# A build-time clock that decides where constant products fill TensorE's gaps: busy share against array-weighted activity

## The chip, the cores and the metric

The kernel runs on one core of a Trainium2 chip. The metric is device time in microseconds of one execution, lower is better; the times given are medians of several runs.

## The reference

A two-layer encoder trunk runs over two groups of 512 tokens (width 1024, 16 heads of 64) with shared weights, all in float32:

```
for i in range(2):
    xn = rms_norm(x, pre_norm_g[i])
    h  = rwkv7_branch(xn) if i == 0 else natten_branch(xn)
    x  = x + rms_norm(h, post_norm_g[i])

# layer 0: r, k, v, z projections; per direction d (forward, backward):
S_t = S_{t-1} (diag(decay_t) + a_t b_t^T) + v_t k_t^T ;  y_t = S_t r_t
out = (group_norm(y_fwd + y_bwd) + bonus) * silu(z) @ w_o
# layer 1: q, k, v, z = xn @ w_in + b_in; attention over a window of 8 x 16 grid tokens
# with a learned relative bias; (o * silu(z)) @ w_o + b_o
```

The inputs are two activations of 512 x 1024 and the weights; the outputs are two activations of the same shape.

## The kernel before

Each 1024 x 1024 matrix is worked off as 8 columns of 8 blocks of 128 x 128 against 512 tokens. To keep float32 accuracy on a faster product, weights and activations are each split into a high part (a cast on ACT) and a low part (a subtraction on DVE), and each block is multiplied three times (lines 802 to 804 in the scan phase, 423 to 425 in the other two).

The program has three stages in time. A prelude normalises both groups, forms the shifted inputs and multiplies the first columns. The scan phase (`scan_phase`, line 1641) runs the recurrence of layer 0 in chunks of 64 tokens for 8 pairs of head groups, 64 steps in all, together with the rest of layer 0's columns and the first of layer 1's. The last stage (`rest`, line 1745) is attention and output.

In the scan phase the recurrence needs many small products. A step (`step`, line 1135) reads the state and the chunk in 64 x 64 products (lines 1162, 1168), copies Z on ACT (1174), solves with the inverse (1189), copies X (1201), and forms the next state and the output in 128 x 64 products (1209, 1213). The factors of the next step are 64 x 64 products too (1068, 1090). For every pair of head groups `prep` (line 823) forms the chunk operands, with two 128 x 128 products for each of four small matrices (872, 873) and Gram products of 64 x 32 (951), and `inverse` (line 975) inverts triangular blocks on DVE and joins them with products of 32 x 32 (lines 1025 and 1027, 64 in a group). Transposes (680, 1288) and sums (646, 1278) use 128 rows.

The order of instructions on TensorE, DVE and ACT in the scan phase is not left to the compiler. `weave` (line 1600) holds a list of generators, "threads": the step, its factors, the loads, the columns (`flow`, line 698), `prep`, `inverse`, `finish` (line 1237). Each yields the engine that it needs next and a function that says when its operands are ready. A class `Clock` keeps a model of time for each engine: every instruction that a thread issues is passed to `note`, which advances its engine and books when its outputs are made. Among the threads that are open and ready within 60 ns (`EPS`) `weave` takes the one of the lowest rank (the step is 0, the columns' products 9), lets it issue up to its next yield, and repeats. Times in this model come from formulas such as `0.4375 * n + 3` ns for a product of n columns in the split format and `1.73 * n + 1` for a full float32 one.

Where no thread is ready, `weave` may put a filler: a product of two constants, the identity (128 x 128) and 256 columns of a constant table, into a part of PSUM that nothing reads (`self.spare`, line 1154). The filler is on line 1626. Three conditions hold for it: no thread is ready, the next TensorE work of any open thread is over `WARM` = 300 ns away in the model, and `Clock.cool` says that TensorE did little in the last 3413 ns of model time. `Clock.busy` then books 440 ns for it. The model is only used at build time; on the chip the filler is an ordinary instruction in TensorE's order.

`cool` sums the intervals in the list `Clock.work`. Two places feed the list: `busy` for fillers, and `weave` after every step of a thread that moved TensorE's time, with the interval from its time before the step to the end of its last product. The tiles of the array are modelled in `matmul`: a product of fewer rows or columns than 128 has a `tile_size` and a `tile_position`, and two products run side by side if they share the column position and differ in the row position.

## Time and profile before

| | |
|---|---|
| median of 3 runs | 1694.72 us (1691.98 to 1698.94) |
| profiled execution, its own time | 1691.19 us |
| its span, first to last instruction | 1689.4 us |
| mean granted TensorE clock | 0.971 |
| TensorE busy | 1572.3 us (93%), 18820 products |
| fillers (line 1626) | 196 |

The profile is of one execution. PE is TensorE's products, PEld its weight loads, DVE the vector engine, ACT the scalar engine, POOL GpSimd, SP the engine that issues the DMAs. "Granted clock" is the share of full speed at which TensorE was clocked in a stretch. Rows of groups give the line, the engine, what is written from what, the shape, how often, then the busy time and the mean of one in nanoseconds, then the idle time of the engine before them and what ended it.

### The profile page before, as it was taken

The numbers are of one execution on the slowest core, as the hardware profiler recorded it, in microseconds if no ns is written. First come the engines' busy times: TensorE is split into PE (matmuls) and PEld (weight loads), VectorE is DVE, ScalarE is ACT, GpSimd is POOL, SyncE is SP. The second block draws the span as 40 slices with busy tenths as digits, with TensorE's granted clock in tenths as the row PEclk, the third lists the DMA queues.
The fourth block names the chain that finished last, engine by engine and source line by source line (L and its number), as shares of the span: only waits on it lengthen the run. The fifth ranks groups of instructions, "written<-read, shape, count | busy, mean of one in ns | idle before, by whom it ended". The sixth has DMA issues, their size and how long they took to land. (4 is left out here: it accounts for less than half of the span.)

```text
span 1689.4 us, 46296 instructions
## 1 busy us (share of the span) xinstructions
PE 1572.3 (93%) x18820; PEld 1201.0 (71%) x18820; DVE 1229.1 (73%) x2725; ACT 982.1 (58%) x1977; POOL 24.2 (1%) x94
## 2 busy tenths in 40 slices
PE   7989888899988998989988999999999898999998
PEld 5767666676766766767766767777787687777776
DVE  8985668689678787887888888745676766465564
ACT  5443655677765768656566665444676655555562
POOL 0000000000000000000000000000000000000000
PEclk9989999899999999999998999999999899999999
DMA  5435678688587787775776765554765246545553
GB/s 208 162 125 187 202 231 260 181 253 267 183 262 229 215 263 238 229 245 181 231 254 209 220 206 165 171 186 138 269 205 172 86 124 240 189 149 176 167 176 106
DMA packets 240821, 336.26 MB, mean 199 GB/s; under 512 B 53696, under 2 KB 119360, under 8 KB 240608
## 3 DMA queue, kind: packets, MB, share of 16 engines
q1 hardware_dynamic: 240608, 333.31, 61.9%
q8 instruction: 148, 2.42, 0.6%
q14 instruction: 65, 0.53, 0.1%
HBM read 227.71 MB, written 105.51 MB: 197 GB/s over the span
## 5 line engine op out<-in xcount | busy, mean ns | idle before, releaser
L802 PE MATMUL pm<-act,whi 128*128 128x512 f32 x640 | 284.9, 445 | 17.2 <-ACT act L747 4.3
L804 PE MATMUL pm<-act,wlo 128*128 128x512 f32 x640 | 258.0, 403 | 10.0 <-DVE wlo L723 9.9
L803 PE MATMUL pm<-act,whi 128*128 128x512 f32 x640 | 258.4, 404 | 7.4 <-DVE act L749 6.4
L423 PE MATMUL pg<-act,whi 128*128 128x512 f32 x448 | 184.0, 412 | 3.1 <-ACT os L1494 1.9
L424 PE MATMUL pg<-act,whi 128*128 128x512 f32 x448 | 179.2, 400 | 4.8 <-DVE act L373 4.8
L425 PE MATMUL pg<-act,wlo 128*128 128x512 f32 x448 | 179.0, 399 | 0.0
L372 ACT CAST whi<-raw 128x512 fp32r<-128x512 f32 x148 | 91.3, 618 | 131.1 <-PE pg L424 87.2
L802 PEld LDWEIGHTS pm<-act,whi 128*128 128x128 f32 x640 | 122.8, 192 | 62.2 <-issue 11.5
L804 PEld LDWEIGHTS pm<-act,wlo 128*128 128x128 f32 x640 | 123.4, 193 | 42.2 <-DVE wlo L723 15.1
L803 PEld LDWEIGHTS pm<-act,whi 128*128 128x128 f32 x640 | 123.5, 193 | 33.3 <-DVE act L749 12.4
L373 DVE TENSOR_TENSOR wlo<-raw,whi 128x512 fp32r<-128x512 f32 x148 | 101.7, 689 | 61.7 <-ACT whi L372 56.2
L723 DVE TENSOR_TENSOR wlo<-raw,whi 128x512 fp32r<-128x512 f32 x160 | 109.1, 685 | 36.5 <-ACT whi L721 33.2
L721 ACT CAST whi<-raw 128x512 fp32r<-128x512 f32 x160 | 98.4, 617 | 58.1 <-PE pm L803 27.5
L424 PEld LDWEIGHTS pg<-act,whi 128*128 128x128 f32 x448 | 85.6, 191 | 22.0 <-DVE act L373 5.2
L423 PEld LDWEIGHTS pg<-act,whi 128*128 128x128 f32 x448 | 85.3, 191 | 21.9 <-issue 3.0
L425 PEld LDWEIGHTS pg<-act,wlo 128*128 128x128 f32 x448 | 85.5, 191 | 18.1 <-issue 0.7
L996 DVE TENSOR_TENSOR N<-etmp,N 128x30 f32<-128x30 f32 (+14 forms) x240 | 78.8, 328 | 4.2
L994 DVE TENSOR_TENSOR etmp<-N 128x30 f32<-128x30 f32 (+14 forms) x240 | 78.6, 328 | 4.1
L1448 DVE CUSTOM_DVE_ANT_0 sb<-sc,bias 128x256 f32<-128x256 f32 x128 | 49.9, 420 | 40.3 <-PE pt L1455 26.4
L1451 ACT ACTIVATE sb<-sb,mx 128x256 f32<-128x256 f32 x128 | 64.1, 503 | 11.0 <-DVE mx L1450 10.8
L1090 PE MATMUL pf<-cab 64*64 64x128 f32 (+1 forms) x2048 | 66.3, 265 | 1.9 <-issue 1.9
L1201 ACT COPY X<-us 64x256 f32<-64x256 f32 x128 | 47.0, 367 | 33.3 <-PE zy L1068 30.1
(389 smaller groups left out, 3370.9 us busy)
## 6 DMA issues: line engine op xcount, KB each, us to landing
dab<-ab SPq DMA_DIRECT2D x32, 1024.0 KB
cab<-dab SPq DMA_DIRECT2D x64, 512.0 KB
raw<-in_w_in_dram SPq DMA_DIRECT2D x128, 256.0 KB
bias<-in_rpb_dram SPq DMA_DIRECT2D x32, 384.0 KB
raw<-in_w_z_dram SPq DMA_DIRECT2D x32, 256.0 KB
dz<-tmp SPq DMA_DIRECT2D x32, 256.0 KB
raw<-in_w_k_dram SPq DMA_DIRECT2D x32, 256.0 KB
dk<-tmp SPq DMA_DIRECT2D x32, 256.0 KB
```

The source lines that it names most:

```text
L372: self.nc.scalar.copy(hi, src)
L373: (eng or self.nc.vector).tensor_tensor(lo, src, hi.bitcast(F32), op=ALU.subtract)
L423: nc.tensor.matmul(ps, hi, x[k][0], start=(k == 0), stop=False)
L424: nc.tensor.matmul(ps, hi, x[k][1], start=False, stop=False)
L425: nc.tensor.matmul(ps, lo, x[k][0], start=False, stop=(k == KT - 1))
L721: nc.scalar.copy(hi, raw[h])
L723: nc.vector.tensor_tensor(lo, raw.pop(h), hi.bitcast(F32), op=ALU.subtract)
L802: nc.tensor.matmul(ps, hi[:, at], xh, start=(k == 0), stop=False)
L803: nc.tensor.matmul(ps, hi[:, at], xl, start=False, stop=False)
L804: nc.tensor.matmul(ps, lo[:, at], xh, start=False, stop=(k == KT - 1))
L994: vt.tensor_tensor(tv, N[:, q + 1:, q:q + 1].broadcast_to([P, n, q]), N[:, q:q + 1, :q].broadcast_to([P, n, q]), op=ALU.mult)
L996: vt.tensor_tensor(N[:, q + 1:, :q], tv, N[:, q + 1:, :q], op=ALU.add)
```

## The change

Three places change. `Clock.matmul` now books every modelled product in `work` with its start, its end and the share of the 128 x 128 array that its tile uses. `Clock.cool` sums the part of each interval that lies in the last 3413 ns, up to now, times that share, and compares the sum with 0.6 of 3413 ns instead of 0.7. A filler is booked with share 1. `weave` no longer books whole steps.

```diff
         self.tiles[tp] = t + c
+        self.work.append((t, t + c, ts[0] * ts[1] / 16384))
         self.t["P"] = t + (13.0 if f32 and not tr else 6.5)
         return t, t + c + self.LAT["P"]
 
-    def cool(self, now, span=3413.0, share=0.7):
-
-        while self.work and self.work[0][1] < now - span:
-            self.work.pop(0)
-        return sum(b - max(a, now - span) for a, b in self.work) < share * span
+    def cool(self, now, span=3413.0, share=0.6):
+
+        self.work = [x for x in self.work if x[1] > now - span]
+        return sum(w * max(min(b, now) - max(a, now - span), 0.0) for a, b, w in self.work) < share * span
...
-        self.work.append((t, t + c))
+        self.work.append((t, t + c, 1.0))
...
             t = best[1]
-            was = ck.t["P"]
             t.step()
             t.end = ck.note() or t.end
-            if ck.pe() > was:
-                ck.work.append((was, ck.pe()))
```

## The prediction

> **What bounds the kernel now.** I read the page's first two parts, then cut the span into its three stages with the table by stretches, then looked for the constant products (the builder's filler, line 1626) and for the stretches at a low clock, and last at the instruction groups and the order of time inside those.

> The first fence is from the page: busy time of the engines, and the granted clock in 40 slices. The second is the table by stretches: length, then PE, weight load, DVE, ACT and POOL busy with counts, then granted clock, DMA share, GB/s.

> ```profile
> PE 1572.3 (93%) x18820; PEld 1201.0 (71%) x18820; DVE 1229.1 (73%) x2725; ACT 982.1 (58%) x1977; POOL 24.2 (1%) x94
> ...
> PEclk9989999899999999999998999999999899999999
> ```

> ```profile
> 0.00:165.00 165.00, 149.48 (x610) 113.96 (x611) 133.64 (x253) 78.29 (x133) 1.85 (x44) 0.96 0.49 167
> 165.00:1173.00 1008.00, 927.00 (x15434) 697.19 (x15433) 781.52 (x1505) 619.40 (x1205) 22.31 (x50) 0.97 0.70 218
> 1173.00:1689.40 516.40, 495.80 (x2779) 389.86 (x2777) 313.95 (x969) 284.39 (x641) 0.00 (x0) 0.98 0.53 172
> ```

> TensorE is the bound: 927.0 of 1008 us in the middle stage, which is the scan phase, the only one that the diff can reach. Two things there are not useful work: 1008 - 927.0 = 81 us in which PE is idle, and a granted clock of 0.97, which is 0.03 x 1008 = 30 us of lost clock. The other two stages keep their instructions and their order.

> Where the fillers stand, by stretch (length, PE busy with their count, clock, DMA share, GB/s), and the group of all 196:

> ```profile
> 165.00:321.00 156.00, 21.55 (x88) 0.94 0.71 224
> ...
> 390.00:402.00 12.00, 3.08 (x12) 1.00 0.74 217
> 402.00:615.00 213.00, 0.00 (x0) 1.00 0.73 226
> 615.00:650.00 35.00, 3.62 (x14) 1.00 0.83 248
> ...
> 733.00:773.00 40.00, 12.40 (x44) 0.91 0.70 224
> ...
> 850.00:920.00 70.00, 9.39 (x38) 0.85 0.71 227
> 920.00:1173.00 253.00, 0.00 (x0) 0.98 0.58 183
> ...
> L1626 PE MATMUL zy<-cc 128*128 128x256 f32 x196 | 50.0, 391 | 0.5 <-ACT Z L1174 0.5
> ```

> They stand in five stretches of 313 us in all; in the rest of the phase the builder saw PE busy and put none. Now the stretches round every drop of the clock in the phase (columns as in the table by stretches):

> ```profile
> 176.90:183.70 6.80, 4.14 (x12) 2.64 (x11) 4.08 (x9) 4.71 (x11) 0.00 (x0) 0.75 0.74 209
> 207.60:214.40 6.80, 4.85 (x75) 3.15 (x75) 5.84 (x9) 2.17 (x5) 0.11 (x1) 0.75 0.66 208
> 286.10:292.90 6.80, 4.13 (x16) 3.03 (x13) 3.77 (x10) 2.21 (x4) 0.00 (x0) 0.75 0.77 218
> ...
> 313.40:327.10 13.70, 13.10 (x243) 10.10 (x247) 5.38 (x8) 10.69 (x21) 0.12 (x1) 0.50 0.70 194
> 658.20:665.00 6.80, 5.24 (x70) 3.88 (x65) 5.49 (x10) 6.24 (x13) 0.12 (x1) 0.75 0.56 157
> 753.80:764.00 10.20, 7.29 (x79) 5.21 (x79) 9.83 (x23) 3.64 (x8) 0.11 (x1) 0.67 0.86 258
> 863.00:873.20 10.20, 8.01 (x29) 5.87 (x28) 7.31 (x16) 3.59 (x8) 0.00 (x0) 0.67 0.65 244
> 900.50:914.20 13.70, 13.50 (x259) 9.97 (x262) 10.67 (x15) 9.14 (x17) 0.00 (x0) 0.50 0.54 160
> 989.30:999.50 10.20, 6.67 (x77) 3.99 (x77) 8.60 (x14) 6.31 (x13) 0.00 (x0) 0.67 0.44 137
> 1098.50:1105.30 6.80, 5.12 (x93) 3.84 (x95) 4.86 (x7) 3.17 (x6) 0.00 (x0) 0.75 0.54 168
> ...
> 501.20:511.40 10.20, 10.20 (x47) 8.38 (x46) 8.02 (x13) 7.84 (x13) 0.11 (x1) 1.00 0.45 139
> ```

> Length times (1 - clock) of the ten rows gives 6.85 twice, 1.7 five times and 3.4 three times: 32.4 us, which is the 30 us again. The reader is to see the two long ones: at 900.5 PE is busy 13.50 of 13.70 us and yet runs at half clock all through, while at 501.2 it is busy 10.20 of 10.20 at full clock. What differs is the kind of product:

> ```profile
> L1027 PE MATMUL pm<-MT,NA 32*32 32x32 f32 x128 | 3.8, 237 | 0.0
> L803 PE MATMUL pm<-act,whi 128*128 128x512 f32 x4 | 2.6, 653 | 0.3 <-DVE act L773 0.3
> ...
> L1025 PE MATMUL pm<-NA,Go 32*32 32x32 f32 x64 | 1.9, 237 | 0.0
> ```

> These are three groups of 900.5 to 914.2: 192 products of 32 x 32, that is 1/16 of the array each. So this trace supports the premise of the change: busy time does not hold the clock up, use of the array does.

> **The change part by part.** (a) What a product counts. Before, a scheduled step counts from its start to PE's end, in full. After, each product counts its modelled duration times rows x columns / 16384, so the blocks of the inverse (lines 1025, 1027) count 1/16, the Grams (line 951, 64 x 32) 1/8, the scan's 64 x 64 products 1/4 and its 128 x 64 ones 1/2. Products of different rows and one column run side by side in the model, two at a time, so a second filled with 64 x 64 blocks counts at most 1/2, below the new 0.6: in any modelled gap of over 300 ns after such work the builder now sees "cool" at once. (b) The threshold: 0.6 x 3413 = 2048 ns in place of 0.7 x 3413 = 2389 ns. In a gap between full-array products, fillers go at a steady 0.6 instead of 0.7, so 1/7 fewer: 28 of the 196, if all stood in such gaps. I expect both together to give 180 to 270 fillers, with new ones beside the inverse and in the steps.

> What a filler costs: in the order of time (start, duration, group),

> ```profile
> 304.95 1.20 PE L1025 MATMUL pm<-NA,Go 32*32 32x32 f32 x64
> ...
> 316.25 1.92 PE L1027 MATMUL pm<-MT,NA 32*32 32x32 f32 x64
> ...
> 747.50 4.58 PE L1626 MATMUL zy<-cc 128*128 128x256 f32 x20
> 755.21 0.85 PE L951 MATMUL pf<-ab 64*32 64x64 f32 x64 [3.12 <-DVE ab L916]
> ```

> 20 fillers took 4.58 us with one tail, (4.58 - 0.38) / 19 = 0.22 us each at full clock, while the builder books 0.44. It puts one only where it sees PE wait over 0.3 us, so a filler whose gap is real costs nothing: the wait covers it, as the 3.12 us behind those 20 shows. If the gap is not there on the chip it costs 0.22 us, 0.44 at half clock.

> (1) Gain where small products hold the clock down: 313.4, 658.2, 900.5 and 1098.5, together 6.85 + 1.7 + 6.85 + 1.7 = 17.1 us of clock. The block of 64 that took 1.20 us at full clock took 1.92 at half. But a faster PE meets the next engine: ACT is busy 10.69 of 13.70 at 313.4, DVE 10.67 of 13.70 at 900.5, ACT 6.24 of 6.80 at 658.2. So the most that these four can give is 3.0 + 0.6 + 3.0 + 1.7 = 8.3 us; the least is 0. At 900.5 the builder books its three blocks of 64 at full clock, where the chip took 1.92 us for each, so it must have seen PE wait there and found itself warm by busy share. With weights it does not. I take two thirds: -5.5 us.

> (2) The other six drops (176.9, 207.6, 286.1, 753.8, 863.0, 989.3; 15.3 us of clock) follow gaps of PE rather than small products. A filler more or less decides them, and there the lower threshold puts fewer. Bounds: none goes, and each of the five stretches with fillers loses one further window of 3.4 us (1.7 us of clock as at 176.9), +8.5; or all go, -15.3. Between, nearest to the first, as 20 fillers at 747.5 did not stop the drop behind them: I take +1.0.

> For the third term, the copy of Z in each step and the longest of TensorE's waits at the steps' own lines (who waited for whom: us, times, longest):

> ```profile
> L1174 ACT COPY Z<-zy 128x256 f32<-128x256 f32 x64 | 23.7, 370 | 48.5 <-PE zy L1168 45.9 <-PE zy L1162 2.4
> ...
> PE us L1209 <- ACT X L1201: 3.0, 5, 1.4
> ```

> (3) New fillers ahead of work that was ready. The steps are a chain of 64 (first row), and a filler set in one of their gaps is in PE's queue ahead of the step's own products. Who waits for those: the copies of Z and X on ACT, the state on DVE, and then the next step. Least 0, most one in each step, 64 x 0.22 = 14 us. The wait in the second row (3.0 us in five times) is the largest that the chip has of such gaps at the steps' own lines, five in 64 steps, so few are asked for: I take +0.5.

> (4) Order. A filler moves the builder's clock by 0.44 us, and from there on other threads may be picked; no instruction but fillers is added, and the loads keep their order within each thread, though they may be issued earlier or later against PE's products. This is not readable from the trace. Of the 81 us of idle PE I allow a tenth either way, 8 us, and take 0, as nothing gives it a sign.

> Sum: -5.5 + 1.0 + 0.5 + 0 = -4.0 us. The profiled execution took 1691.19 us (span 1689.4 and 1.8 round it), so 1687.2 for one like it. The median of the three runs is 1694.72, 3.5 above, so 1690.7 against that; I say 1689, between the two. A measurement of this kernel tells about 0.5% (8.5 us) from no change, and 4 us lies inside.

> [...]

> **The rivals.** *The clock comes back more widely.* New fillers sit beside the inverse and the Grams in the starved stretches and also save part of the six other drops: the whole 8.3 us and a third of 15.3, 13.4 us in all, about 1681. For it: at 753.8 and 989.3 there are 79 and 77 products, mostly small ones that no longer count. Against: DVE is busy 9.83 of 10.20 and 8.60 of 10.20 there, so not all of that clock is time.

> *Slower: fillers in the step chain.* In 402 to 615 and 920 to 1173 there was not one filler, with clocks of 1.00 and 0.98, so nearly nothing to win. There the steps' small products now count a half at most and the builder, wherever it believes that PE waits for Z, X or S over 0.3 us, puts one. If its waits are longer than the chip's in most of the 64 steps, each costs 0.22 us and pushes the next step back. With (1) at a third of its price and (2) at +3, 40 such fillers give 8.8 - 1.8 + 3 = +10, 1705, and 64 give +15, 1710; it decides, over 8.5 us, from 33 on. Against: products of projections fill those stretches, so "nothing ready" is rare there.

> *Only idle windows count.* Then no filler beside busy work does anything and the rest of the sum stands: +1.5, 1696. The row at 900.5 speaks against it, so 0.05. [...]

> *The change does next to nothing:* the two thresholds cancel and about as many fillers stand in about the same gaps. Within 3 us of 1694.7. Against: the blocks weigh 1/16 in place of 1.

> **How the numbers follow.** Forecast (1689, inside 0.5%) 0.34; wide recovery 0.33, nearly all of it faster; slower by the chain 0.20; idle windows 0.05 and nothing 0.08, both inside but for the spread of (4). Of the forecast's 0.34, 0.04 may end over 8.5 us faster by (4), and of the inside cases 0.03 over 8.5 slower. Faster 0.36, same 0.41, slower 0.23. The range: down to all of (1) and nine tenths of (2), 8.3 + 13.8 = 22 below 1694.7, 1673; up to 50 fillers in the chain, 11 - 1.8 + 3 = 12.2 us above it, 1707. The forecast's own range is 1681 to 1697, (4) on either side.

> **What would show it.** Right: fillers of line 1626 between the blocks near 313 and 900 and a granted clock there well above 0.50; a clock of the scan phase of 0.98 or more; fewer fillers in the long runs such as the 20 at 747.5; the two stages around it as long as before. (3) shows as fillers in 402 to 615 and 920 to 1173 directly ahead of lines 1162, 1189 or 1209. Wrong: a clock of 0.97 or less with more fillers; or a middle stage that moves by over 8 us with the clock unchanged, which would be the order.

## The result and the profile after

The change makes the kernel slower, by 0.6 to 0.8%. In its first comparison it takes 1707.52 us (median of 8) against 1692.49 us, ratio 1.0082 with a 95% interval of 1.0057 to 1.0108; two further sessions gave 1.0055 (1.0032 to 1.0078) and 1.0059 (1.0038 to 1.0081). The forecast was 1689 us, 0.3% faster; the range ended at 1707. The profiled execution is the quickest of the eight: 1699.04 us, span 1697.0.

The page of the changed kernel, busy time and granted clock:

```profile
PE 1565.3 (92%) x18798; PEld 1195.4 (70%) x18798; DVE 1229.4 (72%) x2725; ACT 982.3 (58%) x1977; POOL 24.1 (1%) x94
...
PEclk9989999999999999999999999999999899999999
```

The table by stretches, with the columns of before:

```profile
165.00:1173.00 1008.00, 912.60 (x15380) 686.08 (x15379) 777.24 (x1498) 617.36 (x1201) 22.29 (x50) 0.97 0.69 217
...
402.00:850.00 448.00, 405.68 (x7459) 303.23 (x7457) 347.73 (x673) 285.91 (x564) 9.40 (x24) 0.97 0.71 224
```

In the same 1008 us PE is now idle for 1008 - 912.60 = 95.4 us instead of 81, with the same clock of 0.97. Over the whole span (span less PE busy) idle time grew by 14.6 us, from 117.1 to 131.7, and busy time fell by 7.0, from 1572.3 to 1565.3; together that is the 7.6 us between the spans of 1689.4 and 1697.0. Two further profiles of the changed kernel, with spans of 1699.3 and 1694.8 us, have 126.8 and 125.0 us of idle time, so the loss shows as idle time in all three, but its size differs from one execution to the next. Of the 14.4 us in this stage 11.1 lie between 402 and 850, where before had this row (idle 31.2 us, now 42.3; clock 0.99, now 0.97):

```profile
402.00:850.00 448.00, 416.83 (x7611) 312.51 (x7611) 361.35 (x706) 294.30 (x582) 9.49 (x25) 0.99 0.74 229
```

The fillers of line 1626 in the changed kernel, by stretch (length, busy with count, clock, DMA share, GB/s), and their group:

```profile
165.00:321.00 156.00, 18.56 (x66) 0.96 0.70 224
...
402.00:615.00 213.00, 7.23 (x30) 0.97 0.67 215
615.00:650.00 35.00, 5.87 (x14) 0.90 0.69 206
...
733.00:773.00 40.00, 0.59 (x2) 1.00 0.75 239
...
850.00:920.00 70.00, 11.29 (x38) 0.95 0.77 252
...
L1626 PE MATMUL zy<-cc 128*128 128x256 f32 x174 | 50.5, 427 | 0.0
```

Each filler leaves two records: the builder puts 98 fillers into the kernel before and 87 into the changed one, and the 196 in the table of before counts records. There are fewer records, 174 for 196, and yet 50.5 us for 50.0: the mean record takes 427 ns instead of 391. Of their time, from each record's start to the next one, 11.8 of 44.2 us are at half clock, in before 2.7 of 44.5. Now the places of the old drops, and the new ones:

```profile
306.50:313.30 6.80, 6.80 (x75) 5.65 (x68) 4.03 (x7) 4.79 (x7) 2.00 (x3) 0.50 0.56 145
310.00:327.10 17.10, 15.58 (x361) 12.18 (x359) 8.54 (x14) 13.99 (x29) 0.11 (x1) 0.90 0.59 171
...
477.00:487.00 10.00, 6.99 (x153) 5.48 (x153) 5.19 (x12) 4.53 (x10) 0.00 (x0) 0.83 0.89 302
535.00:548.00 13.00, 9.63 (x142) 7.53 (x142) 8.35 (x14) 6.69 (x10) 1.89 (x2) 0.74 0.41 136
634.00:648.00 14.00, 11.38 (x155) 8.44 (x153) 8.20 (x12) 11.47 (x18) 2.00 (x3) 0.76 0.43 132
709.00:723.00 14.00, 7.46 (x140) 5.67 (x130) 7.55 (x17) 5.62 (x13) 0.00 (x0) 0.76 0.98 301
...
900.50:914.20 13.70, 11.33 (x191) 8.67 (x193) 12.48 (x16) 8.50 (x13) 1.89 (x2) 0.88 0.77 267
...
1098.50:1105.30 6.80, 6.80 (x127) 5.40 (x121) 4.95 (x7) 6.61 (x11) 1.90 (x2) 1.00 0.40 128
```

Where before ran at half clock with PE busy, the clock is now 0.90, 0.88 and 1.00. Near 313 the half clock has not gone, though: it comes earlier and is half as long (first row). And the clock drops in four stretches (477 to 723) in which before stood at 1.00, and in each of them PE is idle for 2.6 to 6.5 us; 429 to 440 and 815 to 825, at 1.00 before, have 0.84 and 0.83. The same order without any filler (below) has 0.79, 0.87, 0.83 and 0.71 in those four, so the fillers did not make these drops; they did not prevent them either. In order of time (start, duration, group) the reader sees both kinds of filler:

```profile
307.97 4.64 PE L1626 MATMUL zy<-cc 128*128 128x256 f32 x10
...
904.01 3.48 PE L1626 MATMUL zy<-cc 128*128 128x256 f32 x8
...
908.56 2.43 PE L1626 MATMUL zy<-cc 128*128 128x256 f32 x10
```

Ten records took 4.64 us at 308 and 2.43 us at 909: the first stand in a stretch already cold, that is, at half clock (0.50 from 306.5 to 313.3), and so do the eight at 904 (0.50 from 904 to 907.2).

### The profile page after: what moved, and what is told of

Its sections match the earlier page's. It is cut to its first block, busy times and chain, and to the rows that moved or that the text cites. A ratio compares the mean times of both kernels' runs of the same rounds, so it can differ in the third digit from the quotient of the medians.

```text
span 1697.0 us, 46258 instructions
## 1 busy us (share of the span) xinstructions
PE 1565.3 (92%) x18798; PEld 1195.4 (70%) x18798; DVE 1229.4 (72%) x2725; ACT 982.3 (58%) x1977; POOL 24.1 (1%) x94
## 5 line engine op out<-in xcount | busy, mean ns | idle before, releaser
L803 PE MATMUL pm<-act,whi 128*128 128x512 f32 x640 | 256.1, 400 | 9.2 <-DVE act L749 7.4
L803 PEld LDWEIGHTS pm<-act,whi 128*128 128x128 f32 x640 | 122.9, 192 | 33.4 <-DVE act L749 11.3
L1201 ACT COPY X<-us 64x256 f32<-64x256 f32 x128 | 46.9, 366 | 29.9 <-PE zy L1068 28.4
```

Of the source, the lines that this page charges most:

```text
L803: nc.tensor.matmul(ps, hi[:, at], xl, start=False, stop=False)
```

## The experiments

In the code cuts `...` marks what is left out, and comments explain. A ratio is the time over that of the kernel before, from runs side by side.

The first theory was **order**: other booked times give another order of the real work. The rivals were **clock** (87 fillers keep the clock up less than 98), **in the way** (the new fillers delay ready work), and, as results came in, **cover** (a filler pays where PE is idle anyhow and costs where it is not).

**The two orders without fillers.** In both kernels the fillers were booked in the builder's model and not issued, so the order of everything else is kept:

```diff
-                self.nc.tensor.matmul(self.spare, self.ident, self.scan[0][:, 0:256], ...)
                 ck.busy((128, 128), 440.0)
```

> The order of before, word for word, but the 98 constant products are booked in the builder's model and not issued. Theory 'order' (the change is slower because other booked times give another order of the real work, about 8 us more, and the fillers' own effect is small): 1692 +- 6, the clock near 0.965. Theory 'clock' (fillers are worth time through the granted clock, and after lost it by having 87 instead of 98): clearly slower than before, by 15 us or more, with a mean clock of 0.94 to 0.95.

> The order of after, with its 87 constant products booked but not issued. Theory 'order': slower than the order of before without fillers by the same 0.8% (about 14 us), as nothing but the order differs. Theory 'clock': the same as the order of before without fillers within 5 us, as neither has a filler.

Measured: 1.0060 of before (1.0037 to 1.0082; median 1702.55) for the order of before, and 1.0055 (1.0033 to 1.0076; 1700.4) for the order of after. The theory of order falls as it was put: without fillers neither order is the better one. The theory of clock has the sign right, but with 0.021 less of clock (a mean of 0.947 against 0.968 in the same session) the time is 0.6% longer, not 15 us. In the window from 165 to 1180 the four kernels have these rows, in the order before, before without, after, after without:

```profile
165.00:1180.00 1015.00, 934.00 (x15466) 702.73 (x15465) 784.92 (x1510) 621.24 (x1207) 22.31 (x50) 0.97 0.70 218
```

```profile
165.00:1180.00 1015.00, 904.97 (x15208) 672.55 (x15207) 777.23 (x1499) 618.69 (x1202) 22.33 (x50) 0.92 0.67 215
```

```profile
165.00:1180.00 1015.00, 919.60 (x15411) 691.81 (x15410) 781.71 (x1505) 619.33 (x1204) 22.29 (x50) 0.97 0.69 217
```

```profile
165.00:1180.00 1015.00, 900.31 (x15214) 672.68 (x15213) 779.32 (x1500) 617.45 (x1200) 22.34 (x50) 0.93 0.67 215
```

Idle PE time is 1015 less the busy time: 110.0 us falls to 81.0 by the fillers of before, and 114.7 to 95.4 by those of after. About as much filler time (50.0 and 50.5 us busy) thus took the place of 29.0 us of idle time in one kernel and of 19.3 us in the other. Each row is one execution. With the further profiles on record (151.2 and 149.5 us of idle time in the whole span of after without fillers, 131.7, 126.8 and 125.0 with them) the fillers of after take 18 to 26 us, those of before 27.6 (144.7 to 117.1) in the one pair that there is. So how much less idle time those of after take is not settled.

What fillers do for the clock can be seen where the order is the same. In order: after with fillers and after without, both round the 256 products of 32 x 32 of one `inverse` (lines 1025 and 1027) and the same 12 products of columns; then before without fillers, in the longest stretch at half clock that it has:

```profile
907.20:920.90 13.70, 11.96 (x304) 9.24 (x305) 10.64 (x16) 11.53 (x19) 1.89 (x2) 1.00 0.57 182
```

```profile
910.00:927.00 17.00, 14.07 (x268) 10.45 (x269) 13.94 (x20) 11.43 (x18) 1.89 (x2) 0.50 0.57 180
```

```profile
761.30:792.00 30.70, 21.69 (x287) 14.00 (x289) 19.17 (x34) 14.93 (x27) 2.00 (x3) 0.50 0.64 209
```

With 16 filler records in the stretch the clock is 1.00, without them 0.50, though PE is busy for much the same share of it (11.96 of 13.70 us, 14.07 of 17.00); a second profile without fillers gives 0.50 too (909.5 to 926), the two others with fillers 0.90 and 0.91. Near 313 it is not so: without fillers 192 of the 256 blocks run at 1.00 as well (319.5 to 328), so there it was the other order that took them out of the half clock. And before, with 22 fillers between 733 and 773, has 6.8 us of half clock there (757.2 to 764.0) where the same order without any has 30.7 us.

**The halves of the change.**

```diff
-    def cool(self, now, span=3413.0, share=0.6):      # weighted, as in the change
+    def cool(self, now, span=3413.0, share=0.7):
```

> Half of the change: products weighted by their part of the array, but the threshold left at 0.7; 130 constant products instead of 98 (87 in after). Theory 'clock by threshold' (after is slow since 0.6 puts fewer fillers): back to before or faster, 1685 to 1693, clock 0.975 or more. Theory 'fillers in the way' (weights put fillers ahead of the step's products): slower than after, 1712 or more. Theory 'order': anywhere in 1685 to 1710, not tied to the clock.

```diff
-    def cool(self, now, span=3413.0, share=0.7):      # busy share, as before
+    def cool(self, now, span=3413.0, share=0.6):
```

> The other half: the busy share of before, with the threshold at 0.6; 64 constant products instead of 98. Theory 'clock by threshold': slower than before by 10 us or more and slower than after, since fewer fillers than in either, clock 0.96 or less. Theory 'fillers in the way': faster than before. Theory 'order': anywhere in 1685 to 1710, not tied to the clock.

Measured: the weights with 0.7 give 0.9935 (0.9906 to 0.9965; 1681.52 us), with a mean clock of 0.979, faster than the range of every theory, the nearest being clock; the busy share with 0.6 gives 1.0000 (0.9982 to 1.0019), with 64 fillers and a mean clock of 0.966. Neither half is slow. So 64 fillers do as well as 98 in another order, which speaks against the number alone, and against the clock by threshold, which asked for 10 us more.

**The changed kernel's fillers, split.** On the order of after, all 87 booked, the issue depends on the old rule, computed beside the new:

```diff
+                if ck.idle(now):           # busy share under 0.7; "not" in the second kernel
                     self.nc.tensor.matmul(self.spare, ...)
```

> The changed kernel once more, unedited, on the chip of the three beside it. All theories: about 1.008 of before (1702 to 1709) with a clock near 0.965. If it comes out at 1.005 or less, the 7 us between it and its own order without fillers were a matter of session and not of the fillers.

> The order of after, with its 87 booked fillers, of which only those 54 are issued at which the busy share of before was under 0.7 too. Theory 'in the way' (the 33 that only the weights let in delay ready work): 1690 to 1696, 4 to 10 us faster than the order of after without fillers (1700.4), at a clock near 0.96. Theory 'all alike' (a filler of after gives back in TensorE time what it gains in clock): 1700 to 1707 as with none or all.

> The order of after, with only the other 33 fillers issued: those that the weights let in where the busy share was 0.7 or more. Theory 'in the way': slower than the order without fillers, 1704 to 1712, with a clock little above its 0.947. Theory 'all alike': 1700 to 1707. [...]

Measured: all 87 1.0055 (1703.87 us), the 54 alone 1.0105 (1.0075 to 1.0135; 1711.07), the 33 alone 1.0077 (1.0047 to 1.0108; 1706.78). In the way falls: without the 33 it is slower, not faster. The worth of fillers does not add up: each subset is no better than none (1.0055, and 1.0072 in a later session), the 54 alone even slower, and the two together are no worse than either. In the trace of the 33 the mean record is longest of all, as 11.0 of their 20.4 us (from each record's start to the next one) are at half clock:

```profile
L1634 PE MATMUL zy<-cc 128*128 128x256 f32 x66 | 23.3, 493 | 0.0
```

**The other side of 0.7.** The weighted rule at 0.8, with 136 fillers, and its order without them:

```diff
-    def cool(self, now, span=3413.0, share=0.6):
+    def cool(self, now, span=3413.0, share=0.8):
```

> Weighted shares with the threshold at 0.8; 136 fillers (130 at 0.7, 87 at 0.6). Theory 'more clock, less time': near the 0.7 version, 1678 to 1690, clock 0.975 or more. Theory 'order' (the 0.7 version had a lucky order): 1690 to 1705 at the same clock.

> The order that the weighted share at 0.8 gives, with its 136 fillers booked but not issued. Theory 'order' (its 1.8% over before come from another order of the real work): 1668 to 1680, clearly faster than the two other orders without fillers (1700 and 1702). Theory 'fillers' (they come from idle time filled and clock kept): 1698 to 1704 as the other two, with idle TensorE time of 137 to 144 us and a clock near 0.945.

Measured: 0.9816 (0.9787 to 0.9845; 1662.49 us), below the range of both theories and faster than both kernels of this case; its order without a filler 0.9883 (0.9861 to 0.9905; 1672.27), as the theory of order expected. Against the order of before without fillers (1.0060) that is 2.4%, about 41 us: 1.8% or 30 us from the order, and 0.7% or 11 us from its fillers. The rows of the window, with fillers and without:

```profile
165.00:1180.00 1015.00, 958.63 (x15638) 726.80 (x15637) 794.89 (x1534) 626.58 (x1220) 22.27 (x50) 0.98 0.71 223
```

```profile
165.00:1180.00 1015.00, 919.23 (x15332) 690.17 (x15331) 791.54 (x1521) 625.40 (x1217) 22.27 (x50) 0.94 0.70 220
```

Here the fillers take 39.4 us of idle time (95.8 to 56.4), and their mean record is as short as in before:

```profile
L1626 PE MATMUL zy<-cc 128*128 128x256 f32 x272 | 70.6, 391 | 2.1 <-DVE y L1230 1.6 <-ACT Z L1174 0.5
```

**Each filler twice.**

```diff
                 self.nc.tensor.matmul(self.spare, self.ident, ...)
+                self.nc.tensor.matmul(self.spare, self.ident, ...)
                 ck.busy((128, 128), 440.0)
```

> The order of before, each of its 98 fillers issued twice: 86 us of filler instead of 44 where the builder books 0.44 us. Theory 'cover' (a filler pays where TensorE is idle anyhow, and costs where it is not): the second ones find half as much idle time, so of their 42 us at least 25 are added, less at most 10 us of clock: 1705 or more. Theory 'too few' (the clock is what limits): 1680 to 1692, clock 0.978 or more.

> The order of after, each of its 87 fillers issued twice. Theory 'cover': 1712 or more, and more above after than the doubled before above before, as fewer of its fillers stand over idle time. [...]

Measured: 1.0064 (1.0037 to 1.0091; 1705.1 us) on the order of before with a mean clock of 0.977, 0.008 higher, and 1.0081 (1.0055 to 1.0106; 1707.7) on that of after. The doubled before bears cover out: the clock rose and the time too. The doubled after was expected at 1712 us or more and further above after than the doubled before above before; it is at most 0.26% over after itself (1.0055 to 1.0082 in its three sessions), within the intervals, so that part of the theory is not borne out. The row of the doubled before:

```profile
165.00:1180.00 1015.00, 948.26 (x15576) 726.36 (x15575) 772.75 (x1491) 612.81 (x1194) 22.30 (x50) 0.97 0.68 214
```

Idle time fell by 14.3 us (81.0 to 66.7) for about 40 us of added filler.

**The busy share at 0.8.**

```diff
-    def cool(self, now, span=3413.0, share=0.7):
+    def cool(self, now, span=3413.0, share=0.8):      # busy share, as before
```

> The busy share of before with the threshold at 0.8 instead of 0.7: 125 fillers, close to the 136 of the weighted 0.8. Theory 'number' (what helps is more fillers, however they are chosen): 1662 to 1680. Theory 'weights' (which gaps are chosen matters): 1688 to 1700 with a clock of 0.972 or less. Theory 'order': anywhere from 1665 to 1705, with its idle TensorE time and not its clock deciding.

Measured: 0.9865 (0.9846 to 0.9885; 1671.46 us). Number and order both allow it; weights, as the reason for the gain, do not. Its order was not run without fillers, so the two are not told apart here.

**The fillers of before, split by the new rule.** On the order of before, all 98 booked:

```diff
+                if ck.slack(now):          # weighted share under 0.6; "not" in the second kernel
                     self.nc.tensor.matmul(self.spare, ...)
```

> The order of before, with only those 34 of its 98 fillers issued at which the weighted share was under 0.6 too, that is, which the new rule would let in at the same place. Theory 'choice' (the new rule lets in the poor places): 1700 to 1706, no better than no filler (1.0060). Theory 'any subset' (a filler is worth the same wherever, -0.10 us each): 1697 to 1700. Theory 'low activity is the right sign': 1692 to 1695, most of what the 98 bring.

> The order of before, with the other 64 of the 98 fillers: those that the new rule would not let in, since the weighted share was 0.6 or more. Theory 'choice': 1690 to 1695, all of the gain with two thirds of the fillers. Theory 'any subset': 1695 to 1697. Theory 'low activity is the right sign': 1700 or more.

> The changed kernel unedited, beside its order without fillers on the same chip, to settle what its 87 fillers bring. Earlier it was 1.0082 and 1.0055 of before. All theories that call its fillers worthless: within 0.25% of the run without them. If they are worth as much as in before, 0.6% faster than it.

> The order of after without fillers, again (1.0055 of before in its first session). Expected 1.004 to 1.008; the difference to the run beside it is the worth of the 87 fillers: 0 to +0.25% by 'cover', -0.6% if they work as the 98 of before do.

Measured: the 34 that the new rule allows 1.0058 (1.0036 to 1.0081), no better than none; the other 64 1.0036 (1.0009 to 1.0063); all 98 together are 1.0 by definition, 0.6% under none. The 34 were as "choice" expected, the 64 were not: two thirds of the fillers bring under half of the gain. The interval of the 64 reaches from nearly all of the gain to none of it, so how far the parts fall short of the whole is open. In the trace of the 34 a record takes long as well:

```profile
L1635 PE MATMUL zy<-cc 128*128 128x256 f32 x68 | 22.0, 466 | 0.5 <-ACT Z L1182 0.5
```

Side by side on one chip, after with its fillers is 1.0059 and without 1.0072 (1.0043 to 1.0101): its 87 fillers are worth 0.1%, which these runs cannot tell from nothing.

**The orders of the halves without fillers.**

> The order that the busy share at 0.6 gives, its 64 fillers booked but not issued (with them it is 1.0000 of before). Theory 'order decides' (changing a threshold mainly draws another order, and fillers bring 0 to 10 us): 1692 to 1702, and the orders without fillers then spread over 1672 to 1703. Theory 'fillers decide': 1700 to 1704 as the orders of before and after without them.

> The order that the weighted share at 0.7 gives, its 130 fillers booked but not issued (with them it is 0.9935 of before). Theory 'order decides': 1682 to 1692. Theory 'fillers decide': 1700 to 1704.

Measured: 1.0018 (0.9992 to 1.0045) and 0.9976 (0.9952 to 1.0000; 1690.38 us). Order decides, mostly. All five orders that were run both ways, as ratios to before:

| rule | fillers | without them | with them |
|---|---|---|---|
| busy share 0.7 (before) | 98 | 1.0060 | 1 |
| weighted 0.6 (after) | 87 | 1.0055, 1.0072 | 1.0082, 1.0055, 1.0059 |
| busy share 0.6 | 64 | 1.0018 | 1.0000 |
| weighted 0.7 | 130 | 0.9976 | 0.9935 |
| weighted 0.8 | 136 | 0.9883 | 0.9816 |

Orders differ by 1.9% without one filler; fillers then bring 0 to 0.7%.

## Why the prediction was wrong

**The step that failed is the price of the fillers: "a filler whose gap is real costs nothing", and with it the balance of (1) and (2), -5.5 us for the fillers that come and +1.0 for those that go.** The runs give that balance as a whole. The order of before without fillers is 0.6% slower, so its 98 were worth about 10 us; the order of after without them stands at the same level, and its own 87 bring nothing that shows. The change did not make a worse order, it lost a gain of about 10 us where the sum had 4.5 us won.

Two readings behind the sum were wrong. Each filler leaves two records of 0.22 us, so the 196 records were 98 fillers of 0.44 us, just what the builder books, and the 180 to 270 forecast were 174 records. And (2) was taken near the mild end because "20 fillers at 747.5 did not stop the drop behind them": without any filler the half clock there lasts 30.7 us instead of 6.8, so those fillers earned more than this reading gave them. Nor does a real gap make a filler free: from each record's start to the next one, the fillers of before hold 44.5 us and take away 27.6 us of idle time, so that 17 us, 0.17 us a filler, had to be earned back, as the author reads it by the clock (a mean of 0.968 with them, 0.947 without). Those of after hold 44.2 us and take away 19.6 us, or 18 to 26 by all pairs of profiles. These are net figures: if the higher clock added idle time, it is in them.

**(1), clock where small products hold it down**, was right at one of its two long stretches. At 900 it is the fillers that bring the clock back (1.00 with 16 records, 0.50 without, same order); near 313 the order did it. Busy time alone did not tell the clock: PE was busy 11.96 of 13.70 us at 1.00 and 14.07 of 17.00 at 0.50 in this pair, and 13.50 of 13.70 at 0.50 in before, which speaks against the rival that only idle windows count. That it is use of the array that holds the clock is the author's reading; this pair fits it, and no run tests it apart. What (1) alone is worth in time, no run separates. **(2), the other drops, +1.0**, was mis-sized and misplaced: fillers in plain gaps became not 1/7 fewer but nearly none at 733 to 773 (2 records for 44), and new drops came in stretches without any before, 477 to 723, which the order of after has without fillers too. Over the eight executions the mean clock is 0.966, against 0.968 to 0.970 for before in the later sessions: some 0.003 x 1700 = 5 us of clock lost, where clock was to be won. The clock differs from one execution to the next, 0.963 to 0.972 in those eight, with the profiled one at 0.972 the most favourable; no run shows the reason.

**(3), fillers ahead of the steps, +0.5**: not what happened. 30 and 8 records, 19 fillers, came into 402 to 615 and 920 to 1173. But without the 33 fillers that only the weights let in, 10 records are left there, and the kernel is slower. The slower rival had the sign, not the mechanism. **(4), order, 0 with 8 us either way**: right for this pair by chance, wrong as a bound. Other thresholds of the two rules draw orders that are up to 30 us apart.

What stays open is why the fillers of after are worth less. Half-clocked ones go with it: of filler time 2.7 of 44.5 us is at half clock in before and 11.8 of 44.2 in after (9.5 and 12.4 in its two further profiles), and 2.2 of 61.8 in the weighted 0.8, which gains 0.7%. Both kernels at 0.6 have many (7.3 of 30.9 us with the busy share, worth 0.2%). A filler record at half clock took twice its time, 0.43 us from its start to the next one's instead of 0.215. But it is not useless on that account: in the changed kernel the eight at 904.01 stand ahead of the full clock from 907.20 on. No run changed the half-clocked ones alone, so this is an association and not shown.

## What to carry to other kernels

Before pricing a change to a scheduler's heuristic, run the schedule without what the heuristic inserts: it splits the worth of the inserted work from the worth of the order, and here the orders alone spread over 1.9%. A model that fits one stretch of a trace better, as the weighted share does at 900.5 (PE busy 13.50 of 13.70 us, clock 0.50), does not by itself make a faster kernel; the same weights at 0.8 are 1.8% faster than before and at 0.6 0.7% slower. And filler work is not free because its gap is real: price it by the part of it that idle time covers (27.6 of 44.5 us in before), and at the clock it will run at (0.43 us a record at half clock here, 0.215 at full).
